# Hybrid attention layer on one core: the last output product's first two weight chunks loaded and split earlier, differences before gains, and the last two rows' chains interleaved

## The chip, the cores and the metric

The kernel runs on one core of a Trainium2 chip. The metric is the device time of one execution in microseconds (us), lower is better. The engines are TensorE (PE, matrix products into PSUM banks), VectorE (DVE), ScalarE (ACT), GpSimd (POOL) and SyncE (SP), which here issues nearly all loads and stores. They run side by side, each its own instructions in order, and wait for one another by semaphores.

## The reference

One encoder layer: a normalised input is projected, two attention mixers run side by side, and their gated outputs are projected once, normalised per row and added to the residual. The part around the change is the end:

```python
    for layer in range(DEPTH):
        hn = rmsnorm(h, pre_norm_g[layer])
        proj = jnp.einsum('bld,dc->blc', hn, w_in[layer])
        ...
        y = jnp.einsum('blc,cd->bld', jnp.concatenate([ya, yb], axis=-1), w_out[layer])
        h = h + rmsnorm(y, post_norm_g[layer])

    return h[:, N_META:, :]
```

There are 512 real rows plus 16 meta rows, and `w_out` is 2048 x 2048. The meta rows are dropped before the output projection.

## The kernel before

Products are made nearly in float32: each operand is split into a high part (ACT copies it to float32r, `hi`) and the rest (DVE subtracts, `lo`), and three matmuls of 128x128 by 128x512 make one product of a block. A weight chunk is 128x1024 float32 (512 KB). Its way is: a load by SP into a buffer `st`, the split into `wh` on ACT and into `wl` on DVE, then 12 matmuls on PE. There are three buffers of each kind, so ACT may write the next `wh` only when PE has left one.

The output projection takes the rows as four blocks t = 0 to 3 of 128, and the columns as four blocks g of 512, as two pairs p: (0, 3) and (1, 2). For each pair the 2x2 block product (rows 0-1 and 2-3, two halves of the contraction, two columns) is made by a scheme with seven products instead of eight: its operands are sums and differences (`t1` to `t4` of the mixers' outputs, `ws` of the weights), and the blocks are put together by additions on DVE. A call of `product` goes through four weight chunks, two row blocks u each: 48 matmuls. At the end of the program come, in this order, the second product of both pairs (operand `t2`, function `second`), the third of both (`t3`), and the last of both (`t4`), which adds into the banks (`po`) that the third one filled.

In the last call (`done=end`) the first chunk serves both row blocks; then row 0's bank gets its last three chunks, and then row 1's, so that row 0's bank is complete first. Its four weight chunks come from `wlast(i)` (L757), which splits each in two halves of 512 columns into tiles that are free by then (the high and low parts of the first product's operands were there). The calls of `wlast` stand at the end of the list `todo`, and `fetch` makes them when the last product begins to need them.

For each row block t the end is a chain: the difference of the bank and of what DVE holds in `y[t][2]` (L1072), its square with a sum on ACT (L987), the square root of the whole sum on ACT (L1061), the gain on DVE (L990), the reciprocal (L1077), then four output blocks on DVE (L1066: scale and add the residual `xr`), each with its store. Before that, column block 3 of the row gets the same treatment in `third_done` (difference L1080, square, gain), and POOL makes from its sums the term `ssp` (L1014, L1016) that the square root takes.

A scheduler sets the order of the instructions on each engine. It takes them by priority and by their place in the program; `high_priority` moves the weight splits ahead, `issue_after` holds a piece of work back until a given instruction has been issued, and `keep_in_program_order` (`order`, and every `load`) keeps a sequence as it is written.

Of the kernel before, what the change touches and what calls it, by code (L numbers as in the profile page):

```python
# [10 lines left out]
F32 = mybir.dt.float32  # L11
# [6 lines left out]
P = 128  # L18
# [22 lines left out]
class Lanes:  # L41
# [13 lines left out]
    def mm(self, out, lhsT, rhs, start, stop, **kw):  # L55
        n = int(np.prod(rhs.shape[1:]))
        us = max(n, 256) / 2370.0
        if rhs.dtype == F32:
            us = 4 * max(n, 128) / 2370.0
        self._add(self.nc.tensor.matmul(out, lhsT, rhs, start=start, stop=stop, **kw), us)  # L60
# [45 lines left out]
def kernel(ctx: ExitStack, tc: tile.TileContext, xT, xn, xm, w_s, w_t, w_q, w_o,  # L106
                             gpre, gq, gk, lams, gsub, gpost, ident_d, cos_d, sin_d, dist_d, out):
    nc = tc.nc
# [6 lines left out]
    wp = ctx.enter_context(tc.tile_pool(name="wp", bufs=3))  # L115
    gp = ctx.enter_context(tc.tile_pool(name="gp", bufs=1))
    dr = ctx.enter_context(tc.tile_pool(name="dr", bufs=1, space=DRAM))
    pd = ctx.enter_context(tc.tile_pool(name="pd", bufs=4, space=PSUM))
# [19 lines left out]
    def load(out, in_):  # L138

        tc.keep_in_program_order(nc.sync.dma_start(out=out, in_=in_))  # L140
# [19 lines left out]
    splits = []  # L160

    rank = [AHEAD]
# [14 lines left out]
    def xtile(name, n, dt=F32R):  # L177

        return xp.tile([P, 576], dt, name=name, tag=f"x{n}")
# [29 lines left out]
    def dense_T(segs, pss=None, half=None):  # L209

        pss = pss or [pd.tile([P, 512], F32, name="pd", tag="pd") for _ in segs]
        for k0 in range(0, KT, 8):
            wh, wl = fetch()
            for k in range(k0, k0 + 8):
                c = slice((k - k0) * P, (k - k0 + 1) * P)
                for (n0, n1), ps in zip(segs, pss):
                    three(ps[:, :n1 - n0], wh[:, c], wl[:, c], k, n0, n1)
                    lanes.poll()
                if half and k == 8:
                    half()  # L220
        return pss
# [38 lines left out]
    for t in (TT, 0, 1, 2, 3):  # L260
        rows = P if t < TT else NM
        src = xn[t * P:(t + 1) * P, :] if t < TT else xm
        for j in range(2 if t < 2 else 4):

            tag, w = ("pl", "ph")[j % 2], 1024
            if t >= 2:
                tag, w = ("f", "g", "ql")[t - 2], 512
            st = (gp if tag == "g" else ap).tile([P, w], F32, name="xns", tag=tag,
                                                 bufs=2 if t < 2 else 4)[:rows]
# [63 lines left out]
    def hi(dst, src):  # L333
        nc.scalar.activation(dst, src, AF.Copy)  # L334

    def lo(dst, src, h):
        nc.vector.tensor_tensor(out=dst, in0=src, in1=h.bitcast(F32), op=ALU.subtract)  # L337
# [393 lines left out]
    def block(p, r, c, i):  # L731
        return w_o[PAIRS[p][r], :, 8 * c + 2 * i:8 * c + 2 * i + 2, :]
# [22 lines left out]
    def otile(name, n, dt=F32R):  # L755
        return xtile(name, n, dt)[:, NM:NT]

    def wlast(i):

        st = wp.tile([P, 1024], F32, name="st", tag="st")  # L760
        nc.sync.dma_start(out=st, in_=block(1, 1, 1, i))
        ws = []
        for j in range(2):
            wh, wl = [otile(f"w{x}", 16 + 4 * i + 2 * j + n) for n, x in enumerate("hl")]
            src = st[:, j * 512:(j + 1) * 512]
            with tc.high_priority(rank[0]):
                hi(wh, src)
                lo(wl, src, wh)
            ws.append((wh, wl))
        return ws  # L770
# [9 lines left out]
    pss = dense_T(KEYS, [sc[:, 0, :], sc[:, 1, :]], spread)  # L780
# [12 lines left out]
    v = values(pss)  # L793
# [8 lines left out]
    for h in range(NH):  # L802
# [6 lines left out]
        if h + 1 < NH:  # L809
            if h:  # L810
                weigh(2)
            pss = dense_T(KEYS)
            if h:
                finish_head(h - 1)
            v = values(pss)
# [10 lines left out]
    pss = dense_T(KEYS)  # L826
# [17 lines left out]
    TTv, SUB, ADD = nc.vector.tensor_tensor, ALU.subtract, ALU.add  # L844
# [50 lines left out]
    def banks(pool):  # L895
        return [pool.tile([P, 512], F32, name="po", tag="pd") for _ in range(2)]

    def product(ops, pss, more=False, beside=None, done=None, ahead=2):


        def step(u, i, ws):
            for j in range(2):
                bh, bl = ops(i, j, u)
                c = slice(j * 512, (j + 1) * 512)
                wh, wl = ws[j] if isinstance(ws, list) else [w[:, c] for w in ws]
                mm(pss[u], bh, wh, start=(i + j == 0 and not more), stop=False,
                   skip_group_check=more)
                mm(pss[u], bl, wh, start=False, stop=False, skip_group_check=more)
                mm(pss[u], bh, wl, start=False, stop=(i + j == 4), skip_group_check=more)
                lanes.poll()  # L910

        for i in range(1 if done else 4):
            ws = fetch(ahead)
            for u in range(2):
                step(u, i, ws)
            if beside:
                beside(i)
        if done:
            last = [fetch(len(todo)) for _ in range(3)]
            for u in range(2):  # L920
                for i in range(3):
                    step(u, 1 + i, last[i])
                done(u, pss[u])
        return pss

    def of_t(tiles):
        return lambda i, j, u: [t[:, j, u * P:(u + 1) * P] for t in tiles[i]]


    held = [[product(of_t(b0), banks(pd))]]  # L930
# [6 lines left out]
    yp = ctx.enter_context(tc.tile_pool(name="yp", bufs=1, reuse_waits="tile"))  # L937
    pd2 = ctx.enter_context(tc.tile_pool(name="pd2", bufs=4, space=PSUM, reuse_waits="tile"))
    y = [[yp.tile([P, 512], F32, name=f"y{t}{g}", tag=f"y{t}{g}") for g in range(4)]
         for t in range(TT)]  # L940
    gpB = yp.tile([P, DM], F32, name="gpB")
    pad(yp, "ypad", 256)
    t2, t3 = [operand(n, (yp, yp)) for n in ("t2", "t3")]
# [40 lines left out]
    def square(t, g, src):  # L984
        jk = yp.tile([P, 512], F32, name="jko", tag="jko")
        at = (0, 1, 3, 2)[g]
        return nc.scalar.activation(jk, src, AF.Square, accum_out=ssy[t][:, at:at + 1])  # L987

    def by_gain(t, g, src=None):
        return TTv(out=y[t][g], in0=y[t][g] if src is None else src,  # L990
                   in1=gpB[:, g * 512:(g + 1) * 512], op=ALU.mult)
# [3 lines left out]
    def residual():  # L995
        t, g = places[len(xres)]
        n = len(xres)
        if n < 8:
            x = otile("xr", n, F32)
        else:  # L1000
            x = yp.tile([P, 512], F32, name="xr", tag=f"t2{'hl'[n % 2]}{n // 2 % 4}")
        load(x, xn[t * P:(t + 1) * P, g * 512:(g + 1) * 512])
        xres[t, g] = x
# [7 lines left out]
    def part(t):  # L1011

        p = sspart[t]
        nc.gpsimd.tensor_scalar(out=p, in0=ssy[t][:, 0:1], scalar1=ssy[t][:, 1:2],  # L1014
                                scalar2=ssy[t][:, 2:3], op0=ALU.add, op1=ALU.add)
        nc.gpsimd.tensor_scalar(out=p, in0=p, scalar1=1.0 / DM, scalar2=EPS, op0=ALU.mult,  # L1016
                                op1=ALU.add)
# [12 lines left out]
    def second(p, pool, pb, beside):  # L1030
        r0, r1 = PAIRS[p]
        pss = product(of_t(t2), banks(pool), beside=beside)
        for u, ps in enumerate(pss):
            TTv(out=y[u][r1], in0=ps, in1=y[u][r1], op=ADD)
            TTv(out=y[2 + u][r0], in0=pb[u], in1=y[u][r1], op=ADD)
            square(2 + u, r0, y[2 + u][r0])
            by_gain(2 + u, r0)
            TTv(out=y[2 + u][r1], in0=y[2 + u][r1], in1=y[u][r1], op=ADD)
# [14 lines left out]
    nc.scalar.activation(warm, ssy[1][:, 0:1], AF.Sqrt)  # L1053
    first_half(1, (sum_and_load, sum_and_load))
    second(0, pd, held[0][1], None)
    second(1, pd2, held[1][1], None)
    order = tc.keep_in_program_order

    def row_scale(t):
# [4 lines left out]
    def row_block(t, g):  # L1064
        v = y[t][g]
        order(nc.vector.scalar_tensor_tensor(out=v, in0=v, scalar=ry[t], in1=xres[t, g],  # L1066
                                             op0=ALU.mult, op1=ALU.add))
        load(out[t * P:(t + 1) * P, g * 512:(g + 1) * 512], v)

    def last_block(t, ps):  # L1070
        v = y[t][2]
        order(TTv(out=v, in0=ps, in1=v, op=SUB))  # L1072
        order(square(t, 2, v))
        ry[t] = row_scale(t)
# [1 line left out]
    def turned(t):  # L1076
        order(nc.vector.reciprocal(out=ry[t], in_=ry[t]))  # L1077

    def third_done(t, ps):
        TTv(out=y[t][3], in0=ps, in1=y[t][3], op=SUB)  # L1080
        square(t, 3, y[t][3])
        by_gain(t, 3)
        part(t)

    ry = {}
    third = [product(of_t(t3), banks(pd), beside=lambda i: residual())]
    for u, ps in enumerate(third[0]):
        third_done(2 + u, ps)
    third.append(product(of_t(t3), banks(pd2), beside=lambda i: residual()))
    for u, ps in enumerate(third[1]):  # L1090
        last_block(2 + u, ps)
    for t in (2, 3):
        order(by_gain(t, 2))
        turned(t)
        for g in (0, 3, 1, 2):
            row_block(t, g)
    product(of_t(t4), third[0], more=True, ahead=4)
    for u, ps in enumerate(third[0]):
        third_done(u, ps)

    def end(u, ps):
        last_block(u, ps)
        order(by_gain(u, 2))
        turned(u)
        for g in (0, 3, 1, 2):
            row_block(u, g)

    product(of_t(t4), third[1], more=True, done=end)
# [59 lines left out]
```

## Time and profile before

| what | value |
|---|---|
| median of 3 runs | 919.82 us (919.05 to 920.04) |
| profiled execution | 918.62 us |
| its span, first to last instruction | 916.8 us |
| granted clock of TensorE, mean | 0.997 |
| busy: PE, DVE, ACT, POOL | 900.9, 588.7, 503.3, 121.7 us |

Busy time is not the same as being the limit: DVE is busy for 64% of the span, but what counts is where it is late. A row of a timeline gives the start in us from the span's start, the duration, the engine, the line, the operation and the tiles it writes and reads; `x4` means four such instructions in a row, and what stands in square brackets is the engine's idle time before it and what ended it. Times on PE, DVE and ACT overlap a little from one instruction to the next, so the step from start to start is shorter than a duration.

### The profile page before, as it was taken

Reading aid. Unit: us, or ns where it says so; the run is one execution under the profiler, and the core shown is the slowest. Engines: PE = TensorE matmul, PEld = TensorE weight load, DVE = VectorE, ACT = ScalarE, POOL = GpSimd, SP = SyncE. Lnnn points to the kernel's source line nnn. Section 1 sums busy time; section 2 is a strip of 40 time slices with the busy share of each in tenths; the row PEclk is TensorE's granted clock in tenths of the full one; section 3 lists DMA queues with packets and bytes.
Section 4 is the critical chain, followed back from the end, with each engine's and each line's share of the span. In section 5 each row is a group of like instructions: output and inputs, shape, how many; then the busy total and the mean of one; then the engine's idle time right before and its main releaser. Section 6 shows DMA issues by size and latency. Waiting matters only on the chain.

```text
span 916.8 us, 14275 instructions
## 1 busy us (share of the span) xinstructions
PE 900.9 (98%) x5450; PEld 799.4 (87%) x5450; DVE 588.7 (64%) x1041; ACT 503.3 (55%) x877; POOL 121.7 (13%) x168
## 2 busy tenths in 40 slices
PE   9999999999999999999999999999999999999995
PEld 8999898998989899898997888898888888888884
DVE  6676675747557485675755364785555665776887
ACT  6564564737456374554753435565566565665552
POOL 0102111210201111011010111331111100000012
PEclk9999999999999999999999999999999999999998
DMA  9837646674848558475222332124212228889784
GB/s 339 283 127 208 170 129 160 176 197 131 225 125 229 149 173 215 120 228 130 91 70 73 100 115 69 48 70 149 81 58 93 79 82 286 294 275 320 248 250 174
DMA packets 52979, 149.86 MB, mean 163 GB/s; under 512 B 7920, under 2 KB 14960, under 8 KB 52528
## 3 DMA queue, kind: packets, MB, share of 16 engines
q1 hardware_dynamic: 48160, 132.18, 43.0%
q0 software_dynamic: 4608, 16.78, 10.7%
q8 instruction: 42, 0.69, 0.3%
q14 instruction: 25, 0.20, 0.1%
q10 hardware_dynamic: 144, 0.01, 0.0%
HBM read 140.55 MB, written 41.94 MB: 199 GB/s over the span
## 4 chain that ended last, share of the span: by engine, by line
PE 91%; DVE 5%; ACT 2%; issue 1%; DMA 1%; POOL 0%; DVEq 0%; ACTq 0%; POOLq 0%
PE pd L60 60%; PE po L60 14%; PE sc L60 6%; PE pv L60 5%; PE tr L63 5%; DVE wl L156 1%; DVE y L1066 1%; DMA st<-in_w_o_dram 1%; PE hot L60 0%; PE ss L60 0%; DVE y L990 0%; ACT wh L155 0%; ACT jk L622 0%; DVE l L337 0%; ACT p L603 0%
## 5 line engine op out<-in xcount | busy, mean ns | idle before, releaser
L60 PE MATMUL pd<-xh,wh 128*128 128x264 f32 (+1 forms) x992 | 333.6, 336 | 0.0
L60 PE MATMUL pd<-xl,wh 128*128 128x264 f32 (+1 forms) x992 | 323.4, 326 | 0.0
L60 PE MATMUL pd<-xh,wl 128*128 128x264 f32 (+1 forms) x992 | 323.2, 326 | 0.0
L155 ACT ACTIVATE wh<-st 128x1024 fp32r<-128x1024 f32 (+2 forms) x159 | 165.7, 1042 | 205.9 <-PE pd L60 81.6
L156 DVE TENSOR_TENSOR wl<-st,wh 128x1024 fp32r<-128x1024 f32 (+2 forms) x159 | 191.3, 1203 | 105.0 <-ACT wh L155 103.1
L60 PEld LDWEIGHTS pd<-xh,wl 128*128 128x128 f32 x992 | 186.6, 188 | 16.2 <-DVE wl L156 0.2
L60 PEld LDWEIGHTS pd<-xh,wh 128*128 128x128 f32 x992 | 187.1, 189 | 11.0 <-ACT wh L155 0.2
L60 PEld LDWEIGHTS pd<-xl,wh 128*128 128x128 f32 x992 | 187.5, 189 | 9.4
L509 ACT ACTIVATE p<-p,mx 128x528 f32<-128x528 f32 x64 | 46.9, 733 | 43.2 <-DVE mx L501 42.9
L63 PE MATMUL tr<-ident,p 128*128 128x128 f32 (+1 forms) x320 | 50.6, 272 | 2.8 <-DVE pl L337 2.5
L337 DVE TENSOR_TENSOR pl<-tr,ph 128x512 fp32r<-128x512 f32 x64 | 43.3, 686 | 15.4 <-ACT ph L334 15.1
L501 DVE CUSTOM_DVE_ANT_0 p<-sc,dist 128x528 f32<-128x528 f32 x64 | 44.8, 701 | 11.4 <-PE sc L60 11.0
L60 PE MATMUL pd<-wh,xh 128*128 128x512 f32 x128 | 51.1, 399 | 0.0
L60 PE MATMUL pd<-wl,xh 128*128 128x512 f32 x128 | 50.0, 390 | 0.0
L60 PE MATMUL pd<-wh,xl 128*128 128x512 f32 x128 | 49.9, 390 | 0.0
L334 ACT ACTIVATE ph<-tr 128x512 fp32r<-128x512 f32 x64 | 37.5, 589 | 21.7 <-PE tr L63 21.6
L63 PEld LDWEIGHTS tr<-ident,p 128*128 128x128 f32 (+1 forms) x320 | 36.7, 131 | 13.7 <-DVE pl L337 3.1
L516 DVE SCALAR_TENSOR_TENSOR p<-p,c 128x528 f32<-128x528 f32 x32 | 24.5, 766 | 32.5 <-POOL p L514 32.5
L749 POOL DMA_DIRECT2D ws<-in_w_o_dram x32 | 26.7, 834 | 122.7 <-DMA ws<-in_w_o_dram 67.7
L603 ACT ACTIVATE p<-p,mxA 128x528 f32<-128x528 f32 x32 | 23.5, 736 | 33.8 <-DVE mxA L600 33.7
L514 POOL TENSOR_SCALAR p<-p,sm 128x528 f32<-128x528 f32 x32 | 23.4, 730 | 138.7 <-DVE sm L511 127.7
L605 POOL TENSOR_SCALAR p<-p,smA 128x528 f32<-128x528 f32 x32 | 22.9, 716 | 141.3 <-DVE smA L604 108.1
(221 smaller groups left out, 1591.4 us busy)
## 6 DMA issues: line engine op xcount, KB each, us to landing
st<-in_w_t_dram SPq DMA_DIRECT2D x82, 512.0 KB, 4.4
ws<-in_w_o_dram POOLq DMA_DIRECT2D x32, 512.0 KB, 8.9
st<-ws SPq DMA_DIRECT2D x32, 512.0 KB, 4.0
st<-in_w_o_dram SPq DMA_DIRECT2D x24, 512.0 KB, 4.6
ws<-in_w_o_dram SPq DMA_DIRECT2D x16, 512.0 KB, 6.2
ws<-ws SPq DMA_DIRECT2D x16, 512.0 KB, 5.4
st<-in_w_q_dram SPq DMA_DIRECT2D x16, 512.0 KB, 3.5
xs<-in_xT_dram SPq DMA_DIRECT2D x16, 264.0 KB, 5.4
```

Source lines behind the costliest of these rows:

```text
L60: self._add(self.nc.tensor.matmul(out, lhsT, rhs, start=start, stop=stop, **kw), us)
L63: self._add(self.nc.tensor.transpose(out, in_, ident), 0.109)
L155: splits.append((nc.scalar.activation(wh[:, c], st[:, c], AF.Copy), nc.vector.tensor_tensor(out=wl[:, c], in0=st[:, c], in1=wh[:, c].bitca ...
L156: nc.vector.tensor_tensor(out=wl[:, c], in0=st[:, c], in1=wh[:, c].bitcast(F32), op=ALU.subtract)))
L334: nc.scalar.activation(dst, src, AF.Copy)
L337: nc.vector.tensor_tensor(out=dst, in0=src, in1=h.bitcast(F32), op=ALU.subtract)
L501: nc.vector.tensor_tensor_reduce(out=two(p), in0=sc[:, :, :HALF], in1=two(dist[:, w0:w0 + NT]), scale=-0.125 / slope(h), scalar=3.0e38, op ...
L509: nc.scalar.activation(p2[m], p2[m], AF.Exp, scale=-1.0, bias=mx[:, m:m + 1], accum_out=sm[:, m:m + 1])
L514: nc.gpsimd.tensor_scalar(out=p2[0], in0=p2[0], scalar1=sm[:, 0:1], scalar2=1.0, op0=ALU.mult, op1=ALU.mult)
L516: nc.vector.scalar_tensor_tensor(out=p2[0], in0=p2[1], scalar=c2, in1=p2[0], op0=ALU.mult, op1=ALU.add)
L603: nc.scalar.activation(p, p, AF.Exp, scale=-1.0, bias=mx, accum_out=sm)
L749: nc.gpsimd.dma_start(out=dst, in_=src, accum_op=ALU.add)
```

## The change

The first two chunks of the last product (`wlast(0)` and `wlast(1)`) get buffers of their own, `wr0` and `wr1`. Their loads are issued in the second product of the second pair (`come_early`), and their splits are put among the third products (`split_early`). `wlast` then returns the pieces already split. In `third_done` the differences and squares of both rows stand ahead of the gains and of POOL's term. In `end`, row 0 makes three of its four output blocks, and the fourth comes after row 1's difference and square.

```diff
+    early, early_ws = {}, {}
+
     def wlast(i):
 
-        st = wp.tile([P, 1024], F32, name="st", tag="st")
-        nc.sync.dma_start(out=st, in_=block(1, 1, 1, i))
+        if i in early_ws:
+            return early_ws[i]
+        if i in early:
+            st = early[i]
+        else:
+            st = wp.tile([P, 1024], F32, name="st", tag="st")
+            nc.sync.dma_start(out=st, in_=block(1, 1, 1, i))
         ws = []
         for j in range(2):
             wh, wl = [otile(f"w{x}", 16 + 4 * i + 2 * j + n) for n, x in enumerate("hl")]
             src = st[:, j * 512:(j + 1) * 512]
-            with tc.high_priority(rank[0]):
+            with tc.high_priority(0 if i in early else rank[0]):
                 hi(wh, src)
                 lo(wl, src, wh)
             ws.append((wh, wl))
...
     second(0, pd, held[0][1], None)
-    second(1, pd2, held[1][1], None)
+
+    def come_early(i):
+        if i < 2:
+            early[i] = yp.tile([P, 1024], F32, name="wr", tag=f"wr{i}")
+            load(early[i], block(1, 1, 1, i))
+
+    second(1, pd2, held[1][1], come_early)
...
-    def third_done(t, ps):
-        TTv(out=y[t][3], in0=ps, in1=y[t][3], op=SUB)
-        square(t, 3, y[t][3])
-        by_gain(t, 3)
-        part(t)
-
-    ry = {}
-    third = [product(of_t(t3), banks(pd), beside=lambda i: residual())]
-    for u, ps in enumerate(third[0]):
-        third_done(2 + u, ps)
-    third.append(product(of_t(t3), banks(pd2), beside=lambda i: residual()))
+    def third_done(t0, pss):
+        for u, ps in enumerate(pss):
+            v = y[t0 + u][3]
+            TTv(out=v, in0=ps, in1=v, op=SUB)
+            square(t0 + u, 3, v)
+        for t in (t0, t0 + 1):
+            by_gain(t, 3)
+            part(t)
+
+    def split_early(i):
+
+        with tc.issue_after(splits[-3][0].ins), tc.issue_after(splits[-3][1].ins):
+            early_ws[i] = wlast(i)
+
+    ry, GS = {}, (0, 3, 1, 2)
+    third = [product(of_t(t3), banks(pd), beside=lambda i: (residual(), i == 3 and split_early(0)))]
+    third_done(2, third[0])
+    third.append(product(of_t(t3), banks(pd2),
+                         beside=lambda i: (residual(), i == 1 and split_early(1))))
     for u, ps in enumerate(third[1]):
         last_block(2 + u, ps)
...
     product(of_t(t4), third[0], more=True, ahead=4)
-    for u, ps in enumerate(third[0]):
-        third_done(u, ps)
+    third_done(0, third[0])
 
     def end(u, ps):
         last_block(u, ps)
+
+        if u:
+            row_block(0, GS[3])
         order(by_gain(u, 2))
         turned(u)
-        for g in (0, 3, 1, 2):
+        for g in GS[:4 if u else 3]:
             row_block(u, g)
```

The order on each engine follows from the scheduler. In its rows `y03` is `y[0][3]` (row block 0, column block 3), `po` a PSUM bank, `ssy0` the sums of row 0, and the number behind an underscore tells tiles of one name apart. First the loads, on SP while the second product begins; before:

```order
L148 DMA st_8881<-ws112_582 128x1024
L148 DMA st_8899<-ws113_583 128x1024
L148 DMA st_8917<-ws030_572 128x1024
L148 DMA st_8935<-ws031_573 128x1024
L148 DMA st_8967<-ws032_574 128x1024
```

The same place on SP with the change:

```order
L148 DMA st_8881<-ws112_582 128x1024
L140 DMA wr_8899<-in_w_o_dram 128x1024
L148 DMA st_8901<-ws113_583 128x1024
L140 DMA wr_8919<-in_w_o_dram 128x1024
L148 DMA st_8921<-ws030_572 128x1024
L148 DMA st_8939<-ws031_573 128x1024
L148 DMA st_8971<-ws032_574 128x1024
```

Each of the two loads stands behind a weight load and ahead of the next. On ACT the splits `wh<-wr` come in pairs among the third products, one pair behind each of two weight splits, and on DVE the four `wl<-wr` come one by one among the weight splits and differences there.

Second, DVE from the last row 2 and 3 work to row 0's last difference (`y02`); before:

```order
L337 TENSOR_TENSOR wl_9228<-st_9225,wh_9227 128x512
L337 TENSOR_TENSOR wl_9232<-st_9225,wh_9231 128x512
L1077 RECIPROCAL ssy3_8214<-ssy3_8214 128x1
L1080 TENSOR_TENSOR y03_8180<-po_8965,y03_8180 128x512
L1066 SCALAR_TENSOR_TENSOR y30_8189<-y30_8189,ssy3_8214,xr_8725 128x512
L1066 SCALAR_TENSOR_TENSOR y33_8192<-y33_8192,ssy3_8214,xr_8748 128x512
L1066 SCALAR_TENSOR_TENSOR y31_8190<-y31_8190,ssy3_8214,xr_8768 128x512
L1066 SCALAR_TENSOR_TENSOR y32_8191<-y32_8191,ssy3_8214,xr_8791 128x512
L337 TENSOR_TENSOR wl_9250<-st_9247,wh_9249 128x512
L337 TENSOR_TENSOR wl_9254<-st_9247,wh_9253 128x512
L990 TENSOR_TENSOR y03_8180<-y03_8180,gpB_8193 128x512
L1080 TENSOR_TENSOR y13_8184<-po_8966,y13_8184 128x512
```

The same place on DVE with the change, where the splits of `st_9225` (chunk 2) stand some rows further ahead:

```order
L1079 SCALAR_TENSOR_TENSOR y22_8187<-y22_8187,ssy2_8213,xr_8699 128x512
L997 TENSOR_TENSOR y32_8191<-y32_8191,gpB_8193 128x512
L1090 RECIPROCAL ssy3_8214<-ssy3_8214 128x1
L337 TENSOR_TENSOR wl_9250<-st_9247,wh_9249 128x512
L1079 SCALAR_TENSOR_TENSOR y30_8189<-y30_8189,ssy3_8214,xr_8725 128x512
L1079 SCALAR_TENSOR_TENSOR y33_8192<-y33_8192,ssy3_8214,xr_8748 128x512
L1079 SCALAR_TENSOR_TENSOR y31_8190<-y31_8190,ssy3_8214,xr_8768 128x512
L1079 SCALAR_TENSOR_TENSOR y32_8191<-y32_8191,ssy3_8214,xr_8791 128x512
L337 TENSOR_TENSOR wl_9254<-st_9247,wh_9253 128x512
L1095 TENSOR_TENSOR y03_8180<-po_8969,y03_8180 128x512
L1095 TENSOR_TENSOR y13_8184<-po_8970,y13_8184 128x512
L997 TENSOR_TENSOR y03_8180<-y03_8180,gpB_8193 128x512
```

The splits of chunks 0 and 1 are gone from this place (ahead of these rows DVE has between the weight split `wl_9198` and `y32`'s gain: block `y21`, two splits of chunk 2, block `y22`), one split moved ahead of row 3's blocks, and the two differences now stand side by side behind them.

Third, DVE's last rows, from row 0's reciprocal on; before:

```order
L1077 RECIPROCAL ssy0_8211<-ssy0_8211 128x1
L1066 SCALAR_TENSOR_TENSOR y00_8177<-y00_8177,ssy0_8211,xr_8985 128x512
L1066 SCALAR_TENSOR_TENSOR y03_8180<-y03_8180,ssy0_8211,xr_9005 128x512
L1066 SCALAR_TENSOR_TENSOR y01_8178<-y01_8178,ssy0_8211,xr_9025 128x512
L1066 SCALAR_TENSOR_TENSOR y02_8179<-y02_8179,ssy0_8211,xr_9045 128x512
L1072 TENSOR_TENSOR y12_8183<-po_9060,y12_8183 128x512
L990 TENSOR_TENSOR y12_8183<-y12_8183,gpB_8193 128x512
```

The same rows with the change:

```order
L1090 RECIPROCAL ssy0_8211<-ssy0_8211 128x1
L1079 SCALAR_TENSOR_TENSOR y00_8177<-y00_8177,ssy0_8211,xr_8989 128x512
L1079 SCALAR_TENSOR_TENSOR y03_8180<-y03_8180,ssy0_8211,xr_9009 128x512
L1079 SCALAR_TENSOR_TENSOR y01_8178<-y01_8178,ssy0_8211,xr_9029 128x512
L1085 TENSOR_TENSOR y12_8183<-po_9072,y12_8183 128x512
L1079 SCALAR_TENSOR_TENSOR y02_8179<-y02_8179,ssy0_8211,xr_9049 128x512
L997 TENSOR_TENSOR y12_8183<-y12_8183,gpB_8193 128x512
```

Row 0's fourth output block changed places with row 1's difference. The instructions on PE and on POOL stand in the same order as before.

More of the change, by code (lines that the diff above doesn't have):

```diff
@@ L1094 @@
         turned(t)
-        for g in (0, 3, 1, 2):
+        for g in GS:
             row_block(t, g)
     product(of_t(t4), third[0], more=True, ahead=4)
-    for u, ps in enumerate(third[0]):
-        third_done(u, ps)
+    third_done(0, third[0])
     def end(u, ps):
         last_block(u, ps)
+        if u:
+            row_block(0, GS[3])
         order(by_gain(u, 2))
         turned(u)
-        for g in (0, 3, 1, 2):
+        for g in GS[:4 if u else 3]:
             row_block(u, g)
```

## The prediction

> **What bounds the kernel now.** I read the page first, then the table by stretches for the last 80 us, then the timelines of TensorE (PE), VectorE (DVE), ScalarE (ACT) and SyncE's queue (SPq) in the tail. The span is 916.8 us; the profiled execution took 918.62 us, so 1.82 us lie around the span.
>
> The page's chain that ended last, by engine, and two stretches (length, then busy time and count of PE, weight loads, DVE, ACT, POOL; clock; DMA):
>
> ```profile
> PE 91%; DVE 5%; ACT 2%; issue 1%; DMA 1%; POOL 0%; DVEq 0%; ACTq 0%; POOLq 0%
> 884.00:895.00 11.00, 11.00 (x50) 9.10 (x49) 9.90 (x15) 6.40 (x13) 0.00 (x0) 1.00 0.79 245
> 895.00:906.20 11.20, 11.18 (x50) 8.92 (x48) 9.18 (x17) 4.40 (x11) 4.91 (x4) 1.00 0.35 135
> 906.20:916.80 10.60, 0.00 (x0) 0.00 (x0) 6.74 (x11) 1.02 (x3) 0.00 (x0) 0.75 0.51 198
> ```
>
> PE runs without a gap until 906.2, so nothing that merely makes other engines less busy before then is worth anything. The open part is the 10.6 us behind PE: 6.74 of them DVE work, the rest waits and the last store.
>
> The timeline of PE's last matmul for each of the last two rows, and DVE's rows of the tail (start, duration, idle before and who ended it):
>
> ```profile
> 901.71 0.39 PE L60 MATMUL po<-wl,t4h 128*128 128x512 f32 x1
> 905.79 0.39 PE L60 MATMUL po<-wl,t4h 128*128 128x512 f32 x1
> 889.73 2.49 DVE L337 TENSOR_TENSOR wl<-st,wh 128x512 fp32r<-128x512 f32 x4
> 892.13 1.41 DVE L1066 SCALAR_TENSOR_TENSOR y<-y,ssy,xr 128x512 f32<-128x512 f32 x2
> 893.46 0.68 DVE L990 TENSOR_TENSOR y<-y,gpB 128x512 f32<-128x512 f32 x1
> 895.29 1.29 DVE L337 TENSOR_TENSOR wl<-st,wh 128x512 fp32r<-128x512 f32 x2 [1.14 <-ACT wh L334]
> 896.57 0.67 DVE L1080 TENSOR_TENSOR y<-po,y 128x512 f32<-128x512 f32 x1
> 897.16 2.73 DVE L1066 SCALAR_TENSOR_TENSOR y<-y,ssy,xr 128x512 f32<-128x512 f32 x4
> 899.81 1.28 DVE L337 TENSOR_TENSOR wl<-st,wh 128x512 fp32r<-128x512 f32 x2
> 901.61 0.68 DVE L1080 TENSOR_TENSOR y<-po,y 128x512 f32<-128x512 f32 x1
> 903.15 0.69 DVE L990 TENSOR_TENSOR y<-y,gpB 128x512 f32<-128x512 f32 x1 [0.85 <-ACT jko L987]
> 903.76 0.68 DVE L1072 TENSOR_TENSOR y<-po,y 128x512 f32<-128x512 f32 x1
> 905.29 0.69 DVE L990 TENSOR_TENSOR y<-y,gpB 128x512 f32<-128x512 f32 x1 [0.85 <-ACT jko L987]
> 906.09 2.74 DVE L1066 SCALAR_TENSOR_TENSOR y<-y,ssy,xr 128x512 f32<-128x512 f32 x4
> 908.75 0.68 DVE L1072 TENSOR_TENSOR y<-po,y 128x512 f32<-128x512 f32 x1
> 911.02 2.74 DVE L1066 SCALAR_TENSOR_TENSOR y<-y,ssy,xr 128x512 f32<-128x512 f32 x4
> ```
>
> Row 0's last bank is complete at 901.71+0.39 = 902.10, but its difference (L1072) starts only at 903.76: DVE was still busy with the late splits (L337) and with y13, whose difference came at 901.61 although its product ended 48 matmuls before PE did: at (905.79-901.71)/18 = 0.2267 us each that is 10.9 before 906.18, at 895.3. Row 1's bank is complete at 905.79+0.39 = 906.18, but its difference starts at 908.75, behind row 0's four output blocks. So in the tail DVE, not PE, is late, by 1.66 and 2.57 us. From row 1's first output block (911.02) to the end of the span are 5.78 us: four blocks, the last store's issue, its landing.
>
> How soon DVE can follow PE is seen where DVE was waiting:
>
> ```profile
> 884.03 0.39 PE L60 MATMUL po<-wl,t3h 128*128 128x512 f32 x1
> 884.46 0.69 DVE L1072 TENSOR_TENSOR y<-po,y 128x512 f32<-128x512 f32 x1
> ```
>
> 884.46 is 0.04 after 884.42, so row 0's bank can be taken at 902.14 and row 1's at 906.22.
>
> **The loads moved ahead.** Two loads of 512 KB leave SP's place at 883.86 (and 2.72 later) and go behind two weight loads that SP issues while the second product begins.
>
> ```profile
> 883.86 3.05 SPq L761 DMA_DIRECT2D st<-in_w_o_dram  x2
> 845.77 0.32 SPq L148 DMA_DIRECT2D st<-ws  x1
> 845.77 3.04 SPq L148 DMA_DIRECT2D st<-ws  x2
> 840.00:851.00 11.00, 11.00 (x50) 9.09 (x50) 5.08 (x5) 4.24 (x4) 0.00 (x0) 1.00 0.71 225
> 851.59 1.06 ACT L155 ACTIVATE wh<-st 128x1024 fp32r<-128x1024 f32 x1 [1.66 <-PE po L60]
> DMA to landing us min/median/max: 3.2/3.8/4.9
> ```
>
> The last line is the weight loads' time to landing between 840 and 862. SP issues a weight load at 845.77 and the next at 845.77+3.04-0.32 = 848.49, when a buffer comes free, and each issue takes 0.32: the two new issues fall into SP's own waits and delay no issue. The load issued at 845.77 lands by about 849.6, and ACT takes it at 851.59, held by PE, not by the load: 2.0 us to spare. ACT could start then because PE had left a buffer; two more chunks of 12 matmuls (2.72 each) lie before the new one is used, 5.44 us, of which ACT's 1.06 and DVE's 1.23 are needed: 3.1 us more. So a load may land about 5.1 us late, at 8.9 instead of 3.8, before PE waits. Two extra loads of 512 KB at the 225 GB/s of this stretch are 2.33 us each, 4.7 together; even a load queued behind both stays under 8.9. Cost between 0 and a stall that I price below as a rival; I take 0, the side on which the row of ACT's wait stands.
>
> **The splits moved ahead.** Four splits on ACT and four on DVE go among the third product. Per chunk ACT needs 1.16 us (the pair at 890.13, below), and by the changed order the pairs stand right ahead of these two splits:
>
> ```profile
> 867.96 1.06 ACT L155 ACTIVATE wh<-st 128x1024 fp32r<-128x1024 f32 x1 [1.71 <-PE po L60]
> 873.40 1.06 ACT L155 ACTIVATE wh<-st 128x1024 fp32r<-128x1024 f32 x1 [1.71 <-PE po L60]
> 877.16 1.23 DVE L156 TENSOR_TENSOR wl<-st,wh 128x1024 fp32r<-128x1024 f32 x1 [0.24 <-ACT wh L155]
> 879.88 1.23 DVE L156 TENSOR_TENSOR wl<-st,wh 128x1024 fp32r<-128x1024 f32 x1 [1.50 <-ACT wh L155]
> ```
>
> Each pair fits into 1.71 us of idle. On DVE each split is 0.60 (889.73 to 892.13 for four); the four, 2.4 us, meet small idle times and make the weight splits behind them up to 0.7 late, against the 3.1 us that PE leaves, and the 1.50 at 879.88 absorbs the rest: 0. If that cover were gone, each split would put 0.60 into PE's wait, 2.4 at most.
>
> **DVE after 889.73.** ScalarE's splits of the first two late chunks, and one of its squares:
>
> ```profile
> 888.14 1.14 ACT L334 ACTIVATE wh<-st 128x512 fp32r<-128x512 f32 x2
> 890.13 1.16 ACT L334 ACTIVATE wh<-st 128x512 fp32r<-128x512 f32 x2 [0.85 <-DMA st<-in_w_o_dram]
> 904.53 0.63 ACT L987 ACTIVATE jko<-y 128x512 f32<-128x512 f32 x1 [1.42 <-DVE y L1072]
> ```
>
> Until 889.73 DVE's sequence is as before. Then, by the changed order, in start-to-start times (output block (908.75-906.09)/4 = 0.665, split 0.60, gain and reciprocal 906.09-905.29 = 0.80): block y21 889.73, two splits 890.39, block y22 891.59, gain and reciprocal 892.26, split 893.06, four blocks 893.66, split 896.32, differences y03 and y13 at 896.92 and 897.5. Before, these two stood at 896.57 and 901.61: two chunks (four splits, 2.4 us) are gone, and with them the wait of 1.14. Chunks 2 and 3 take the places of the two loads at 883.86, whose data ACT had at 888.14 and 890.13, early enough for these splits. The gain of y03 follows its difference by 1.53 (903.76 to 905.29) at 898.45, that of y13 one square later (905.29-904.53 = 0.76) at 899.2. DVE is then free from 899.8, and waits for PE until 902.14, **2.3 us to spare**.
>
> **Row 0.** Difference at 902.14 instead of 903.76; the blocks follow by 906.09-903.76 = 2.33, at 904.47. Gain 1.62.
>
> **Row 1.** Its difference now stands behind three blocks: 904.47+3x0.665 = 906.46, which is 0.24 after its bank is ready, so the fourth block queued behind it loses nothing. That block runs while ACT squares, in the 0.8 us that DVE idled. Without the interleaving it would be 907.13. Blocks 911.02-908.75 = 2.27 later: 908.73. Against 911.02 that is **2.29 us earlier**: 1.62 from the first part, 0.67 from the interleaving. The floor set by PE, difference at 906.22, would give 2.53.
>
> **The last store.** The stores keep their spacing of 0.665; their time to landing is
>
> ```profile
> DMA to landing us min/median/max: 2.0/2.1/3.8
> ```
>
> The gap between row 0's last block and row 1's first shrinks, from 911.02-908.83 = 2.2 to about 0.9 us. Bounds: 0 and 3.8-2.1 = 1.7 us; I take 0, since the four blocks at 906.09 were as close behind one another and nothing else is moving by then.
>
> **GpSimd** makes a tiny term that ACT's square root needs:
>
> ```profile
> 898.11 3.67 POOL L1014 TENSOR_SCALAR ssp<-ssy 128x1 f32<-128x1 f32 x1 [19.21 <-ACT jko L987]
> 901.85 0.19 POOL L1016 TENSOR_SCALAR ssp<-ssp 128x1 f32<-128x1 f32 x1
> 903.22 0.86 POOL L1014 TENSOR_SCALAR ssp<-ssy 128x1 f32<-128x1 f32 x1 [1.18 <-ACT jko L987]
> ```
>
> The first operation takes 0.86 to 3.67 us beside DVE work. Started at about 898.5, behind the square of y03, the pair ends by 902.4 at worst, 1.3 us before row 0's square root, which comes when its square ends (902.14+1.53 = 903.67); row 1's term then has until 908. The Trainium skill, SBUF — State Buffer, section Who interferes with whom, says that a VectorE operation with two SBUF inputs and a GpSimd operation that reads SBUF exclude each other, and whichever started first makes the other wait. By that rule GpSimd could also hold up the gain at 898.45. The trace agrees for GpSimd's wait (3.67 against 0.19); the gain at 903.15, beside the 0.86, kept its 0.69, so DVE's wait is not seen.
>
> **Sum.** 918.62-2.29 = 916.33 for an execution like the profiled one. That one lies 1.20 under the median of 919.82 (runs 919.05 to 920.04), and the result is a median: 919.82-2.29 = **917.5**.
>
> **Rivals.**
> - *A smaller gain, 918.3 to 919.5.* Either the last store lands at 3.8, giving back 1.7 (919.2), or GpSimd holds a gain for its 3.67+0.19: 898.45 becomes 902.3, two gains make it 903.5, row 0 starts 1.4 late and 0.9 us are left (918.9). For it: both durations stand in the trace. Against: the 3.8 belongs to stores beside weight loads, and DVE's gains never showed longer than 0.69.
> - *No change, 919.8.* The end is not set by DVE's order, or the chunks left in the late place come as late as before. Against it: both DVE's late starts are followed by rows without any other wait; the changed order does show the moves.
> - *Slower.* The two early loads hold back the weight loads behind them, and PE waits in the second product. It decides where a landing passes 8.9 us, and each us beyond is one of PE; the change is a loss from 11.2 on. Its price, if both took the longest median on the page,
>
> ```profile
> ws<-in_w_o_dram POOLq DMA_DIRECT2D x32, 512.0 KB, 8.9
> ```
>
> is 2x8.9 = 17.8 before the next load's 3.8, so 21.6-8.9 = 12.7 of waiting, less 2.3: 930; half of it, 924. Against it: that queue adds into memory, and loads on SP took at most 4.9 here. The Trainium skill, DMA: Bandwidth & Descriptors, section Queues, rings and completion order, says that each engine takes a ring's descriptors in order, so that a load waits behind the earlier one. By that rule the two waits add up as priced here instead of the rate being shared; no row here shows two loads of this size issued within 0.4 us on SP.
>
> **Numbers.** Forecast 0.76 (916.5 to 918.3), smaller gain 0.12, no change 0.07, slower 0.05. What a measurement can tell from no change is about 0.2%, 1.84 us, so 917.98 is the line: 2.29 is only 0.45 beyond it, and medians of runs that scatter by 1 us leave about a sixth of the forecast on the other side. Faster 0.63, within 0.2% 0.32, slower 0.05. Range 916.4 to 919.2: the forecast and most of the smaller gain.
>
> **What would show it.** Right: PE without a gap to about 906.2; DVE idle before row 0's last difference, released by PE, and that difference within 0.1 of the bank; row 1's first block near 908.7; nearly 8.3 us behind PE's end instead of 10.6. Wrong: a wait of PE for a split or load between 851 and 895; a DVE gain over 0.69 beside GpSimd near 898; a last store that lands later than 2.1.

## The result, and the profile after

| | before | with the change |
|---|---|---|
| median of 8 runs each | 919.02 us (917.83 to 920.04) | 916.56 us (916.14 to 917.77) |
| ratio | | 0.9976, 95% interval 0.9966 to 0.9986 |
| profiled execution, its span | 918.62, 916.8 us | 916.64, 914.7 us |
| end of PE's last matmul | 906.18 | 906.36 |
| row 1's first output block | 911.02 | 908.92 |
| from one to the other | 4.84 | 2.56 |

The kernel is faster by 0.24%, with an interval of 0.14 to 0.34%. PE's work did not move: it ended 0.18 us later in this execution than in the one before, and the time behind it fell from 10.6 to 8.3 us.

The table by stretches of the changed kernel (length, then busy time and count of PE, weight loads, DVE, ACT, POOL; clock; DMA share, GB/s):

```profile
840.00:862.00 22.00, 22.00 (x99) 18.21 (x98) 15.58 (x17) 9.99 (x13) 0.00 (x0) 1.00 0.85 281
895.00:906.20 11.20, 11.20 (x51) 9.06 (x49) 7.62 (x14) 2.46 (x7) 1.90 (x4) 1.00 0.24 94
906.20:914.70 8.50, 0.15 (x1) 0.00 (x0) 5.30 (x9) 1.01 (x3) 0.00 (x0) 0.68 0.64 247
```

The first row is the stretch with the early loads: the DMA engines are busier than the 0.71 and 0.65 of its halves before, and PE is still busy in all of it. In the second, DVE has 7.62 us of work where it had 9.18. The third is the tail.

PE's last matmul of each row, and DVE's timeline of the end, in the changed kernel:

```profile
901.88 0.39 PE L60 MATMUL po<-wl,t4h 128*128 128x512 f32 x1
905.97 0.39 PE L60 MATMUL po<-wl,t4h 128*128 128x512 f32 x1
896.95 1.28 DVE L1095 TENSOR_TENSOR y<-po,y 128x512 f32<-128x512 f32 x2
898.42 1.45 DVE L997 TENSOR_TENSOR y<-y,gpB 128x512 f32<-128x512 f32 x2 [0.19 <-ACT jko L994]
902.31 0.69 DVE L1085 TENSOR_TENSOR y<-po,y 128x512 f32<-128x512 f32 x1 [2.44 <-PE po L60]
903.85 0.69 DVE L997 TENSOR_TENSOR y<-y,gpB 128x512 f32<-128x512 f32 x1 [0.85 <-ACT jko L994]
904.65 2.08 DVE L1079 SCALAR_TENSOR_TENSOR y<-y,ssy,xr 128x512 f32<-128x512 f32 x3
906.65 0.69 DVE L1085 TENSOR_TENSOR y<-po,y 128x512 f32<-128x512 f32 x1
907.25 0.74 DVE L1079 SCALAR_TENSOR_TENSOR y<-y,ssy,xr 128x512 f32<-128x512 f32 x1
908.12 0.69 DVE L997 TENSOR_TENSOR y<-y,gpB 128x512 f32<-128x512 f32 x1
908.92 2.74 DVE L1079 SCALAR_TENSOR_TENSOR y<-y,ssy,xr 128x512 f32<-128x512 f32 x4
```

The row to look at is 902.31: row 0's last difference now follows 2.44 us of idle time that PE ended, 0.04 after the bank's last matmul (901.88+0.39 = 902.27). Row 1's difference at 906.65 is 0.29 after its bank, and row 0's fourth block at 907.25 fills the time in which ACT squares. GpSimd's four operations, which could have been late:

```profile
898.50 0.86 POOL L1021 TENSOR_SCALAR ssp<-ssy 128x1 f32<-128x1 f32 x1 [18.98 <-ACT jko L994]
899.44 0.48 POOL L1023 TENSOR_SCALAR ssp<-ssp 128x1 f32<-128x1 f32 x1
900.02 0.36 POOL L1021 TENSOR_SCALAR ssp<-ssy 128x1 f32<-128x1 f32 x1
900.47 0.19 POOL L1023 TENSOR_SCALAR ssp<-ssp 128x1 f32<-128x1 f32 x1
```

They are done by 900.7, over 3 us before the first square root (903.91).

### The profile page after: what moved, and what is told of

It reads as the page before. It is cut to its first block, busy times and chain, and to the rows that moved or that the text cites. A ratio compares the mean times of both kernels' runs of the same rounds, so it can differ in the third digit from the quotient of the medians.

```text
span 914.7 us, 14275 instructions
## 1 busy us (share of the span) xinstructions
PE 900.8 (98%) x5450; PEld 798.6 (87%) x5450; DVE 588.4 (64%) x1041; ACT 502.7 (55%) x877; POOL 119.2 (13%) x168
## 3 DMA queue, kind: packets, MB, share of 16 engines
q0 software_dynamic: 4608, 16.78, 10.6%
## 4 chain that ended last, share of the span: by engine, by line
PE 92%; DVE 4%; ACT 2%; issue 1%; POOL 0%; DMA 0%; DVEq 0%; ACTq 0%; POOLq 0%
PE pd L60 60%; PE po L60 16%; PE sc L60 6%; PE pv L60 5%; PE tr L63 5%; DVE wl L156 1%; DVE y L1079 0%; PE ss L60 0%; DMA gcol<-in_gpre_dram 0%; ACT jk L622 0%; DVE l L337 0%; ACT p L603 0%; DVE pl L337 0%; POOL ssh L249 0%; ACT wh L155 0%
## 5 line engine op out<-in xcount | busy, mean ns | idle before, releaser
L461 POOL TENSOR_SCALAR pm<-pm 32x256 fp32r<-32x256 f32 x32 | 22.2, 695 | 146.9 <-ACT pm L334 146.5
```

## The experiments

What was open after that: three edits came together, and the trace of the whole doesn't say which of them did the work. An execution's span also moves with what lies before the tail: PE's last matmul ended between 905.81 and 907.87 in the profiles of kernels whose PE instructions are the same. So each run is read by two numbers: the time from PE's last matmul to row 1's first output block in its profile (4.84 before, 2.56 with the change; called the lag below), and the ratio to runs of the kernel before on the same chip, five rounds each. The runs can tell the ratios of the kernels with early chunks (0.9975 to 0.9984, intervals about 0.0009 to either side) from 1, but not from one another. The shares below rest on the lags, each read from one profile.

**The early chunks alone.** The changed kernel with the old `third_done` and the old `end` (the part in `end`):

```diff
...
-        if u:
-            row_block(0, GS[3])
         order(by_gain(u, 2))
         turned(u)
-        for g in GS[:4 if u else 3]:
+        for g in (0, 3, 1, 2):
             row_block(u, g)
```

> The early loads and splits alone, with row 0's four output blocks together again and the old order in the source of third_done. Theory (VectorE was late for row 0 by 1.66 us, the interleaving is worth 0.67 on its own account): row 1's first output block comes 3.2 us after PE's last matmul (4.84 before, 2.56 with the whole change), the span is 1.6 us shorter than before, ratio 0.9982. Rival (the interleaving makes all of the gain): no change, ratio 1.000. Rival (differences ahead of gains carry part of it): less than 1.2 us shorter.

Lag 909.72-906.49 = 3.23, span 915.5, ratio 0.998 (0.9971 to 0.9989). As the theory had it. The step to the whole change, 3.23 to 2.56, is the interleaving: 0.67. The old source order of `third_done` made no difference here: the scheduler had both differences of rows 0 and 1 side by side without that edit, and with the interleaving as well the compiled order on every engine is the changed kernel's row for row, so that kernel wasn't run.

**The interleaving alone**, in the kernel before:

```diff
+        if u:
+            row_block(0, 2)
         order(by_gain(u, 2))
         turned(u)
-        for g in (0, 3, 1, 2):
+        for g in (0, 3, 1, 2)[:4 if u else 3]:
             row_block(u, g)
```

> The interleaving alone: row 0's fourth output block behind row 1's difference, all else as before. Theory: DVE is late by the same 1.66 us for row 0, and row 1 gains one block, 0.67 us: its first output block 4.2 us after PE's last matmul, ratio 0.9993. Rival (the interleaving needs the early splits to be worth anything): 4.84, ratio 1.000. Rival (it makes all of the gain): 2.6, ratio 0.9976.

Lag 909.75-906.24 = 3.51, less than the 4.2 expected; ratio 0.9995 (0.9986 to 1.0004), which can't be told from no change. The lag has a second cause. DVE's and ACT's rows for chunk 2 in this kernel:

```profile
894.68 1.29 DVE L337 TENSOR_TENSOR wl<-st,wh 128x512 fp32r<-128x512 f32 x2 [0.47 <-ACT wh L334]
894.01 1.16 ACT L334 ACTIVATE wh<-st 128x512 fp32r<-128x512 f32 x2 [2.56 <-DMA st<-in_w_o_dram]
```

DVE waited 0.47 us for the late load here, 1.14 in the profile of before: 0.67 of the 1.33 is the landing of one load, the other 0.67 (rounded) the interleaving. This wait differs from execution to execution.

**Differences first alone**, in the kernel before (the two calls follow suit):

```diff
-    def third_done(t, ps):
-        TTv(out=y[t][3], in0=ps, in1=y[t][3], op=SUB)
-        square(t, 3, y[t][3])
-        by_gain(t, 3)
-        part(t)
+    def third_done(t0, pss):
+        for u, ps in enumerate(pss):
+            v = y[t0 + u][3]
+            TTv(out=v, in0=ps, in1=v, op=SUB)
+            square(t0 + u, 3, v)
+        for t in (t0, t0 + 1):
+            by_gain(t, 3)
+            part(t)
...
```

> Only the source order of third_done is changed: both differences ahead of the gains. Theory: DVE takes y13's difference before y03's gain, and no longer idles 0.85 us for the square of y13; 0.6 us of that reach row 0's last difference, so row 1's first output block comes 4.2 us after PE's last matmul, ratio 0.9993; beside the early splits the same edit is worth nothing, since DVE idles there anyway. Rival (the order inside third_done is never on the path): 4.84, ratio 1.000.

Lag 910.08-905.81 = 4.27, ratio 0.9996 (0.9988 to 1.0005). The lag is the theory's; a difference of 0.6 us in 918 is too small for the runs. DVE's two gains in this kernel:

```profile
901.27 0.68 DVE L990 TENSOR_TENSOR y<-y,gpB 128x512 f32<-128x512 f32 x1
902.21 0.69 DVE L990 TENSOR_TENSOR y<-y,gpB 128x512 f32<-128x512 f32 x1 [0.25 <-ACT jko L987]
902.82 0.68 DVE L1072 TENSOR_TENSOR y<-po,y 128x512 f32<-128x512 f32 x1
```

The idle time for y13's square is 0.25 instead of 0.85, and row 0's last difference comes 0.6 earlier. So this edit is worth 0.6 in the old kernel and nothing beside the early chunks.

**Loaded early, split late.** The whole change, but the four splits of the early chunks are held behind the last ordinary weight split, where they were:

```diff
-            with tc.high_priority(0 if i in early else rank[0]):
-                hi(wh, src)
-                lo(wl, src, wh)
+            if i in early:
+                with tc.issue_after(splits[-1][0].ins), tc.issue_after(splits[-1][1].ins), tc.high_priority(rank[0]):
+                    hi(wh, src)
+                    lo(wl, src, wh)
+            else:
+                with tc.high_priority(rank[0]):
+                    hi(wh, src)
+                    lo(wl, src, wh)
...
-                         beside=lambda i: (residual(), i == 1 and split_early(1))))
+                         beside=lambda i: (residual(), None)))
```

> The whole change, but the two early chunks are split where they were before: loaded early, four splits back on DVE between the last products (2.4 us of work). Theory (what matters is whether DVE is free when PE ends row 0's bank, and it had 2.44 us to spare): the spare time is used up to within 0.1 us, row 1's first output block 2.6 to 2.8 us after PE's last matmul, the span within 0.2 us of the changed kernel's, ratio 0.9976 to 0.9979. Rival (the gain is the split work taken off DVE's late stretch): 2.4 us more on DVE show, most of the gain is lost, row 1's first block at 4.0 or later, ratio 0.999.

Lag 908.51-905.95 = 2.56, ratio 0.9975 (0.9966 to 0.9984): the whole gain, without the early splits. Its rows:

```profile
889.49 2.49 DVE L337 TENSOR_TENSOR wl<-wr,wh 128x512 fp32r<-128x512 f32 x4
895.10 0.68 DVE L337 TENSOR_TENSOR wl<-st,wh 128x512 fp32r<-128x512 f32 x1
898.94 1.29 DVE L1100 TENSOR_TENSOR y<-po,y 128x512 f32<-128x512 f32 x2
900.42 1.45 DVE L1002 TENSOR_TENSOR y<-y,gpB 128x512 f32<-128x512 f32 x2 [0.19 <-ACT jko L999]
901.90 0.69 DVE L1090 TENSOR_TENSOR y<-po,y 128x512 f32<-128x512 f32 x1
```

The four splits are back on DVE, and none waits for a load. DVE comes to row 0's last difference at 901.90 with no idle time shown before it, 0.04 after that bank (PE ended at 905.95, row 0's bank 18 matmuls of 0.2267 earlier, 901.86). The gain ahead of it started at 901.18, and DVE's steps are 0.60, so DVE could have been there at 901.78: PE still set the start. The spare time is used up to the last tenth, and costs nothing.

**The early loads alone**, that is the same splits with the old `third_done` and the old `end` as well:

> The early loads alone: splits back among the last products, row 0's four blocks together, old third_done. Theory (the load is what made DVE late): DVE is just free when row 0's bank is complete, row 1's first output block 3.2 to 3.3 us after PE's last matmul, as with the early loads and splits together (3.23), ratio 0.998. Rival (the splits matter too, once the order of the differences is the old one): 0.6 us or more later, 3.8 and up.

Lag 909.66-906.43 = 3.23, ratio 0.9984 (0.9975 to 0.9992): as with the early loads and splits together.

**Everything but the early chunks**: the two edits of order in the kernel before.

> Interleaving and differences first, with the chunks loaded and split as before. Theory (on DVE nothing but the late load and the idle time for y13's square stood between the late splits and row 0's bank): 0.6 us from the order and 0.67 from the interleaving add up, row 1's first output block about 3.6 us after PE's last matmul when ACT's wait for the late load costs DVE the 1.1 us that it did before, and about 2.9 when the load lands 0.7 earlier; 1.0 us of the change is the early load's alone. Ratio about 0.9988. Rival (the two edits of order do the same as the early load): 2.6.

Lag 909.21-906.06 = 3.15, ratio 0.9982 (0.9974 to 0.9991). In this profile the late load cost DVE 0.71 us:

```profile
894.74 1.29 DVE L337 TENSOR_TENSOR wl<-st,wh 128x512 fp32r<-128x512 f32 x2 [0.71 <-ACT wh L334]
```

4.84 less 0.67 (interleaving), 0.60 (order) and 1.14-0.71 = 0.43 (the load) is 3.14. So the two edits of order, which cost no memory and no load, bring 1.27 of the 2.28 us, and the early loads the other 1.01. Taken the other way round, the early loads alone bring 1.61 (4.84 to 3.23) and the interleaving 0.67: the shares depend on which edit comes first.

**All four chunks early.** `wr` for two, and four freed buffers `ts` of half a chunk for the others:

```diff
+        else:
+            early[i] = [gp.tile([P, 512], F32, name="ts", tag="g", bufs=4) for _ in range(2)]
+            for j in range(2):
+                load(early[i][j], block(1, 1, 1, i)[:, j, :])
...
-    third = [product(of_t(t3), banks(pd), beside=lambda i: (residual(), i == 3 and split_early(0)))]
+    third = [product(of_t(t3), banks(pd), beside=lambda i: (residual(), i > 1 and split_early(i - 2)))]
-                         beside=lambda i: (residual(), i == 1 and split_early(1))))
+                         beside=lambda i: (residual(), i < 2 and split_early(2 + i))))
```

> The whole change with all four chunks loaded early and split among the third products, so that twice the bytes go through the second product and no split is left on DVE between the last products. Theory (VectorE only has to be free when row 0's bank is complete): DVE idles about 4.8 us there instead of 2.44, row 1's first output block stays 2.56 us after PE's last matmul, ratio 0.9976 as for the change. Rival (the gain grows with the work taken away): 1 to 2 us more, ratio 0.9955 to 0.9965. Rival (early loads hold back the weight loads): landings over 8.9 us and gaps on PE, the span longer by each gap.

Lag 908.67-906.10 = 2.57, ratio 0.998 (0.9971 to 0.9989). DVE idles longer (4.57 us of the 4.8 expected) and the end does not move:

```profile
902.06 0.69 DVE L1089 TENSOR_TENSOR y<-po,y 128x512 f32<-128x512 f32 x1 [4.57 <-PE po L60]
852.19 1.06 ACT L155 ACTIVATE wh<-st 128x1024 fp32r<-128x1024 f32 x1 [2.33 <-DMA st<-ws]
862.00:884.00 22.00, 22.00 (x99) 18.22 (x98) 21.69 (x30) 15.02 (x24) 4.15 (x4) 1.00 0.85 284
```

In the second row a weight load lands after PE has left the buffer, so that ACT waits for it, 2.33 us instead of the 1.66 that PE makes it wait. Four loads aren't needed for that: with two early loads the longest such wait was 2.4 to 2.6 us in four profiles, though in the changed kernel's own no weight load held ACT up once the early loads were issued. PE shows no gap all the same, and even with DVE busy for 21.69 of 22 us among the third products.

**Splits not held back.** The change without `split_early`: the scheduler puts the splits into the second products.

```diff
-            with tc.high_priority(0 if i in early else rank[0]):
+            with tc.high_priority(rank[0]):
...
-                         beside=lambda i: (residual(), i == 1 and split_early(1))))
+                         beside=lambda i: (residual(), None)))
```

> The change without split_early: the early chunks are still loaded early, and the scheduler may split them as soon as it likes, at the weight splits' own priority, among the second products. Theory (PE has 3 us of margin for each weight split, and nothing else is late there): no gap on PE, row 1's first output block 2.56 us after PE's last matmul, ratio 0.9976. Rival (the hold is needed: ScalarE meets a split whose load has not landed, and the weight splits queued behind it are late): a wait of ACT for wr of over 3 us and a gap on PE, ratio 0.998 or more.

Lag 908.91-906.34 = 2.57, ratio 0.9978 (0.9969 to 0.9987). ACT does meet a split whose load hasn't landed:

```profile
852.94 1.15 ACT L334 ACTIVATE wh<-wr 128x512 fp32r<-128x512 f32 x2 [2.85 <-DMA wr<-in_w_o_dram]
854.00 1.04 ACT L155 ACTIVATE wh<-st 128x1024 fp32r<-128x1024 f32 x1
```

The weight split behind it starts at 854.00 (851.76 in the changed kernel), and PE's margin takes it without a gap.

**The last gain in a tile of its own**, a try at a version that beats the change:

```diff
         order(TTv(out=v, in0=ps, in1=v, op=SUB))
         order(square(t, 2, v))
+        if t < 2:
+            w = early[t][:, :512]
+            order(TTv(out=w, in0=v, in1=gpB[:, 1024:1536], op=ALU.mult))
+            y[t][2] = w
         ry[t] = row_scale(t)
...
-        order(by_gain(u, 2))
         turned(u)
```

> The whole change, and the last gain of rows 0 and 1 is written to a tile of its own (the freed buffers of the early chunks) instead of over the difference, so that it need not wait until ScalarE has squared the difference. Theory (the chain from bank to first output block is now all that lies behind PE): reciprocal waits for the square root instead of the gain, about 0.25 us less for each row, and row 1's difference follows its bank at once: row 1's first output block 2.1 us after PE's last matmul instead of 2.56, ratio 0.9971. Rival (that stretch is set by the output blocks' work on DVE, 4 of them queued): no change, 2.56, ratio 0.9976.

Lag 910.13-907.87 = 2.26, of the 2.1 expected; ratio 0.9978 (0.9969 to 0.9986), not to be told from the change.

```profile
907.95 0.68 DVE L1085 TENSOR_TENSOR y<-po,y 128x512 f32<-128x512 f32 x1
908.67 0.69 DVE L1089 TENSOR_TENSOR wr<-y,gpB 128x512 f32<-128x512 f32 x1
909.28 0.74 DVE L1079 SCALAR_TENSOR_TENSOR wr<-wr,ssy,xr 128x512 f32<-128x512 f32 x1
909.94 0.15 DVE L1094 RECIPROCAL ssy<-ssy 128x1 f32<-128x1 f32 x1
909.48 0.29 ACT L1074 ACTIVATE ssy<-ssy,ssp 128x1 f32<-128x1 f32 x1
```

The square root is ready at 909.77, but DVE is in row 0's fourth block until 909.94. The tail is 0.3 us shorter than the change's; its time is not shown to be.

## Why the prediction was right

- *Where the limit was.* Right: PE waits for nothing from 759 us to its end in either kernel, and DVE's late starts closed, from 1.66 to 0.04 us for row 0 and from 2.57 to 0.29 for row 1. Spare time of DVE before row 0's difference: 2.3 forecast, 2.44 measured.
- *Row 0, row 1 and the sum.* The lag fell by 2.28, forecast 2.29. The span fell by 2.1, because PE ended 0.18 later. The interleaving was put at 0.67, and is 0.67 in the step from the early chunks alone to the whole change. The steps inside came as forecast too: difference to blocks 2.34 us (forecast 2.33), row 1's difference to its first block 2.27 (2.27).
- *The loads.* They cost nothing, as forecast. The two `wr` loads took 6.4 to 6.8 us to land, the weight loads of that stretch 4.4 in the median and up to 5.9, against 3.8 and 4.9 before. The longest is no sign of the early loads by itself: the kernel with the two edits of order and no early load had one of 5.7. The medians are 3.8 to 4.2 in the four profiles without early loads and 4.2 to 4.7 in the six with two. The 2.0 us that the prediction saw between landing and ACT were used up in some profiles (ACT's waits of 2.4 to 2.6 above); what held is PE's margin behind them and the bound of 8.9, also with twice the bytes (7.3 at most). A `wr` load of the changed kernel took some 2.2 us longer than the median weight load. That is near the 2.33 which the prediction gave a load of this size, but no run tells a load that waits behind another from two that share the rate.

The landings in the changed kernel, first the weight loads of 840 to 862, then `wr`:

```profile
DMA to landing us min/median/max: 4.0/4.4/5.9
DMA to landing us min/median/max: 6.4/6.6/6.8
```

- *The splits.* They cost nothing, as forecast. But the sentence that lists the four splits (2.4 us) first among what makes room on DVE gave them a share that they don't have. The room was needed only up to row 0's bank, 1.62 us. The late load's wait (1.14) and the order of the differences (0.60) make 1.74 together, which is enough without them. The sum stayed right because the forecast stopped at PE's bank.
- *Median.* 917.5 forecast, 916.56 measured, only 0.16 inside the lower end of the range. The first three runs of the kernel before lay high (919.82); over eight runs its median is 919.02, and the difference of medians is 2.46 against the 2.29. That the two agree within 0.2 us is partly luck, since the interval of the gain is 1.3 to 3.1 us; the lag is the sharper test.
- *GpSimd and the stores.* No gain was longer than 0.69 beside GpSimd: the pair of 1.45 at 898.42 holds the wait for y13's square. The Trainium skill, SBUF — State Buffer, section Who interferes with whom, lets either of the two wait; in these rows only GpSimd's operations are longer than alone. The first one (L1021) took 0.86 beside a gain and 0.36 at 900.02, where DVE is idle; the second (L1023) 0.48 and 0.19. The prediction's 3.67 against 0.19 compared the first with the second; its own time alone is the 0.36. The last eight stores landed after 2.0 to 2.2 us in both kernels.

## What to carry to other kernels

At the end of a kernel ask when the engine behind the matmuls must be free, not how much work it has: work taken away beyond that instant is worth nothing (four splits here, eight in another run), and edits that each shorten the way to it need not add up. A load that is issued in the busiest stretch can be brought forward to where its queue waits for buffers; its own landing was longer there (6.4 to 6.8 us), so count it against the margin of the transfers beside it. A long tail of equal pieces for one row should let the next row's first step in as soon as its bank is complete.

## What was not expected of the hardware

One load of 512 KB issued among stores cost DVE 0.47, 0.71, 1.14 and 1.17 us in four profiles of kernels with the same instructions up to there: a wait on a late load is a spread, and in none of the profiles with early loads did DVE wait there. Of the difference between two profiled executions, up to 2 us come from where PE ends (905.81 to 907.87). No edit makes that: PE's last 700 matmuls took 156.5 us in ten of the eleven profiles and 156.6 in the changed kernel's, so the difference was there by 751 us, ahead of the first early load. A lag measured from PE's end is steadier (2.56, 2.56, 2.57 and 2.57 in four kernels with the same tail).
